# The convolution's sample tokens: products of overlapping rows on GpSimd and sums on VectorE

## The chip, the cores and the metric

The kernel runs on one core of one Trainium2 chip, as one launch. The metric is the device time of that launch in microseconds; the median of several runs counts.

## What is computed

The reference is one inference step of a decoder of two layers. A prompt of 256 tokens and 8 samples of 8 new tokens each go through the same weights. In each layer four groups of 256 channels mix the tokens in four ways: latent attention over cached pages (A), a convolution module (B), spatial gating (C) and a recurrence (D). An output projection, cross-attention to a memory and a feed-forward network follow. The change touches the convolution of group B:

```python
def conv_module(pb, conv_state, p):
    a, gate = pb[..., :CONV_DIM], pb[..., CONV_DIM:]
    glu = a * jax.nn.sigmoid(gate)
    xin = jnp.concatenate([conv_state.astype(glu.dtype), glu], axis=1)
    y = lax.conv_general_dilated(xin, p['conv_w'].astype(xin.dtype)[:, None, :],
                                 window_strides=(1,), padding='VALID',
                                 dimension_numbers=('NWC', 'WIO', 'NWC'),
                                 feature_group_count=CONV_DIM)
    y = y + p['conv_b']
    ...
```

It is depthwise, causal and 31 taps wide. For a sample, xin holds 30 old columns of its state and the 8 new ones, so 38 columns give 8 results per channel.

## The kernel before

Channels lie on the 128 partitions, so the 256 channels of the convolution are two tiles, and the tokens lie along the free dimension: 256 prompt columns and 8 x 8 sample columns, NT = 320 in all. `conv_dense` (line 965) projects and gates. For each of the two tiles it fills `xp`, the prompt's columns with 30 zeros ahead, and `xq`, 8 samples of 38 columns, of which the first 30 come by a DMA of the state (line 972) that depends on nothing else, and the last 8 from the gate. `yi` takes the results. All three are parts of one buffer that the profile calls Bkeep.

`conv` (line 990) is a generator. For each tile it makes 31 steps. A step is one VectorE instruction over the prompt's 256 columns, out of the helper `stt` (line 401), that adds tap k times the shifted `xp` to `yi`, and one over the 64 sample columns (line 1000) that does the same for `xq`. Each of these needs the one before it, since both add into the same columns. The condition `k % 4 < 0` on line 1000 never holds, so all of them are VectorE's. The helper `tt` (line 397) is the plain two-input operation on either engine. `red` (line 416) is a VectorE sum over the last axis, and `hold` says that an instruction is not scheduled ahead of another, without a wait.

The steps of `conv` are run in portions of ten between the steps of `mla_sample` (line 1298), which scores the cached pages of group A. In eight steps that function loads four tiles of pages (Sckt), casts them on ScalarE (Sckh), takes the rest on GpSimd (Sckl, through line 397), multiplies on TensorE (pS, pZ) and goes through a softmax on VectorE (Sra, Sz, Asm). GpSimd also issues indirect DMAs of the page rows (Scb, line 1326). This part of the kernel is called the scoring stage below; it lies at about 205 to 320 us in the first layer and 885 to 1020 us in the second. The convolution's rest (transposes, normalisation, a projection) follows later in the same stage.

The order of each engine's instructions comes from the framework's scheduler. It knows dependences by the columns that an instruction touches, so a tap that reads none of the 8 new columns of `xq` can be placed ahead of the gate. Engines work their queues in order. Each buffer has a fixed count of copies, listed in `BUFS`.

Of the kernel before, what the change touches and what calls it, by code (L numbers as in the profile page):

```python
# [23 lines left out]
NT = 320  # L24
# [297 lines left out]
def body(nc, tc, a, nl=L):  # L322
# [14 lines left out]
                Ckeep=1, Ccv=1, Ck2=2, Csm=4, Ch=2,  # L337
                Bkeep=1, Bms=1, Bf=4, Bg1=4, Bk2=2, Bsm=6, Bh=2, Mm=2, MkT=1, Mvm=2, Mf=2, Mma=1, Mk2=2, Msm=2, Mrw=1)
    PBUFS = dict(D=3, R=2, A=2, S=3, Z=2, K=2, E=2, X=3, Y=2)
# [18 lines left out]
    def block(tag, n):  # L358
        """one tile for what lives as long; returns what hands out its columns"""
        t, used = sb(tag, [128, n]), [0]  # L360

        def take(*shape):
            w = math.prod(shape)
            v = t[:, used[0] : used[0] + w]
            used[0] += w
            assert used[0] <= n
            if len(shape) == 1:
                return v
            d = "abc"[: len(shape)]
            return v.rearrange("p (%s) -> p %s" % (" ".join(d), " ".join(d)), **dict(zip(d, shape)))  # L370

        return take
# [7 lines left out]
    def in_order(first, last):  # L380
        """keeps the streamed products in program order among themselves"""
        after(first, dense_last[0])
        dense_last[0] = last
# [3 lines left out]
    def hold(ins, prev):  # L387
        """not before prev, by the schedule alone"""
        if prev is not None:
            tc.add_manual_dep(ins.ins, prev.ins.name, LATER, reason="held back")  # L390
# [43 lines left out]
    def keep(n):  # L434
        """columns held for the whole launch"""
        o = fixed[0]
        fixed[0] += n
        return fix[:, o : o + n]
# [26 lines left out]
    def rsq(e, now=False):  # L465
        """e <- e ** -0.5"""
        p, n = e.shape
        if n <= 12 and not now:
            tt(e, e, C("mhalf")[:p, :n], ALU.pow, G)
            return  # L470
        z, t = sb("nw", [128, 64]), sb("nw", [128, 64])
        z, t = z[:p, :n], t[:p, :n]
        ts(z.bitcast(I32), e.bitcast(I32), -0.5, 1597463007.0)
        for it in range(3):
            tt(t, z, z, MUL)
            stt(t, t, -0.5, e, MUL, MUL)
            stt(z if it < 2 else e, t, 1.5, z, ADD, MUL)

    def split(hi, lo, src, scale=None, eng=None):
        """hi + lo = src * scale, both in fp32r"""  # L480
        if scale is None:
            S.copy(hi, src)  # L482
            tt(lo, src, hi.bitcast(F32), SUB, eng)
        else:
            act(hi, src, scale=scale)
            stt(lo, src, scale, hi.bitcast(F32), MUL, SUB)

    def halves(raw, spans, scales=None, pool=()):
        """raw: a loaded tile, spans: column ranges -> (hi, lo) for each"""
        out = []  # L490
        per = 512 // (spans[0][1] - spans[0][0])
        for k0 in range(0, len(spans), per):
            part = spans[k0 : k0 + per]
            hi, lo = sb("wh", [128, 512], F32R), sb("wl", [128, 512], F32R)
            c0, c1 = part[0][0], part[-1][1]
            if scales is None:
                split(hi[:, : c1 - c0], lo[:, : c1 - c0], raw[:, c0:c1], None, G if k0 // per in pool else V)
            for n, (a0, a1) in enumerate(part):
                v = slice(a0 - c0, a1 - c0)
                if scales is not None:  # L500
                    split(hi[:, v], lo[:, v], raw[:, a0:a1], scales[k0 + n])
                out.append((hi[:, v], lo[:, v]))
        return out

    def wload(l, nm, idx, K):
        """one chunk of weights: a list of (hi, lo) [128, C] for its K row tiles"""
        o, n = OFFS[(nm, idx)]
        cols = n // K
        raw = sb("wr", [128, 1024])
        nc.sync.dma_start(raw[:, :n], a["w"][l, o : o + 128 * n].rearrange("(p c) -> p c", p=128))  # L510
        return halves(raw, [(k * cols, k * cols + cols) for k in range(K)], None, POOLED.get(nm, ()))
# [77 lines left out]
    def late():  # L589
        """what the first products do not need"""  # L590
        nc.scalar.dma_start(cst[:, EARLY:], a["cst"][:, EARLY:KEPT])
        nc.scalar.dma_start(pti, a["ptab"])
        nc.scalar.dma_start(pt1, a["pt1"])
        for l in range(nl):
            ts(idx[l], pti, 64.0, float(l * 32))
            V.tensor_scalar(out=idx[l], in0=idx[l], scalar1=C("kr"), scalar2=None, op0=ADD)

    def group_norm_T(oj, vec, g, tag="F"):
        """oj: token rows [128, 256] x 3 -> split transposes of the normalised, scaled rows, [128, 2, NT] x 2"""
        r = small(3, 1.0)  # L600
# [7 lines left out]
        out = []  # L608
# [9 lines left out]
    def layernorm64(yj, eps):  # L618
        """per token and 64 columns, in place, without gain"""
        mn, vr = small(12, 0.0), small(12, 1.0)  # L620
# [47 lines left out]
    def rwkv(l, xs, vec):  # L668
# [44 lines left out]
        G.tensor_copy(pT[:, :, 4:12], P[:, :, 263:NT:8])  # L713
        # normalised removal key
        kp = sb("u", [128, 2, NT])
# [24 lines left out]
        stt(b1, ta, 1.0, kk, ADD, MUL)  # L740
        # bonus
        bon = take(12)
# [18 lines left out]
        flat = lambda ap: ap.rearrange("p x t -> p (x t)")  # L761
        # token rows of v, b and k
        UV = [sb("u", [128, 5, 2, 64]) for _ in range(2)]
# [14 lines left out]
        for i in range(2):  # L778
# [11 lines left out]
            gate = S.copy(BKt[i][:, 0:4], p.rearrange("p (c t) -> p c t", c=4))  # L790
        # products between steps of a chunk
        GM = [[sb("u", [128, 5, 128]) for _ in range(2)] for _ in range(2)]
# [13 lines left out]
        for hf in range(2):  # L806
# [4 lines left out]
            for i in range(2):  # L811
                tt(GM[i][hf][:, 4], p[:, i * 128 : i * 128 + 128], mask("mgso" if hf else "mgse"), MUL)
                tt(N[2][R, i, R], GM[i][hf][R, 4, R], ident[R, R], ADD)
        # inverse of the unit triangular blocks by doubling
        v3d = lambda p, n: p[:, : n * 128].rearrange("p (c t) -> p c t", c=n)
# [18 lines left out]
        for lev in (2, 4, 8, 16, 32):  # L834
# [4 lines left out]
            for q in qs:  # L839
# [4 lines left out]
                product(p, Lt[q], Gt[q], n)  # L844
                # the blocks of this level: rows of the first halves, columns of the second
                m = bm(mask("lev%d" % lev), n).rearrange("p n (b x t) -> p n b x t", x=2, t=lev)[:, :, :, 1]
# [17 lines left out]
        lng, lnb = rload(l, ("ln_g", "ln_b"), sb("ln", [128, 512]), back[-1])  # L864
        # state, chunk by chunk
        y = [take(256) for _ in range(3)]
# [77 lines left out]
    def rwkv_out(l, vec, y, lng, lnb, vt, bon, tg, g2):  # L944
        # head norm, bonus, gate
        layernorm64(y, 64e-5)
# [12 lines left out]
    def sigmoid(t, scale=1.0, src=None):  # L959
        """t <- 1 / (1 + exp(scale * src))"""  # L960
        act(t, t if src is None else src, AF.Exp, scale=scale)
# [28 lines left out]
    def conv(l, xpq, vec):  # L990
        (pw,) = mload(l, ("pw",), sb("ms", [128, 512]))
        y = []
        for i, (xp, xq, yi) in enumerate(xpq):
            wc = lambda k: VE(vec, "conv_w", i * 31 + k)
            cb = VE(vec, "conv_b", i)
            ts(yi[:, :256], xp[:, 0:256], wc(0), cb)
            ts(e8(yi[:, 256:NT]), xq[:, :, 0:8], wc(0), cb)
            for k in range(1, 31):
                stt(yi[:, :256], xp[:, k : k + 256], wc(k), yi[:, :256], MUL, ADD)
                (G if k % 4 < 0 else V).scalar_tensor_tensor(out=e8(yi[:, 256:NT]), in0=xq[:, :, k : k + 8], scalar=wc(k), in1=e8(yi[:, 256:NT]), op0=MUL, op1=ADD)  # L1000
                yield
            y.append(yi)
        yj = []
# [98 lines left out]
    def mla(l, pj, vec):  # L1102
# [39 lines left out]
        G.tensor_copy(ckn[LO], pj[2][LO, 192:320])  # L1142
        # queries, keys and values
        rq = take(36)
# [32 lines left out]
        for j in (2, 0, 1):  # L1177
# [24 lines left out]
            else:  # L1202
# [7 lines left out]
                S.copy(kpT[0:32], p[0:32, 256:320])  # L1210
        # sample queries against latents
        qp, qz = take(8, 4, 8), take(8, 4, 32)
# [67 lines left out]
    class Side:  # L1280
        """work that is put between the steps of another"""

# [15 lines left out]
    def mla_sample(l, vec, t, side):  # L1298
# [12 lines left out]
        def scan(g, Q):  # L1311
            """page rows, and their scores without the rotary part"""
            ch[0] = "S"
# [145 lines left out]
    def mem_proj(l, vec, nm, Ms):  # L1459
        """the memory's keys or values; Ms holds its split parts once they are made"""  # L1460
        out = [sb("m" if nm == "wk" else "vm", [128, 512]) for _ in range(2)]
# [76 lines left out]
    def xattn(l, vec, kTm, vm, ahead, nxt):  # L1538
# [4 lines left out]
        for t in qpad:  # L1543
            hold(G.memset(t, 0.0), early)
        # queries without their norms; the sums of squares carry both epsilons
        qT, us = [], sb("m", [128, 2, 4, 4, 8])
# [3 lines left out]
        def scale(c0, n):  # L1550
            """1 / the norms of the queries, with the softmax's factor"""
            r = rs[:, c0 : c0 + n]
# [21 lines left out]
        def sample():  # L1574
# [6 lines left out]
            for g in range(2):  # L1581
# [28 lines left out]
                p = ps("F")  # L1610
                # each head's rows of its own transpose, 128 columns apart
                for h in range(4):
# [154 lines left out]
```

## Time and profile before

| | |
|---|---|
| median of 3 runs | 1382.19 us (1376.61 to 1384.05) |
| span of the profiled execution | 1383.1 us (no time apart from the span is listed) |
| TensorE busy | 1330.9 us, 96% |
| VectorE busy | 962.2 us, 70% |
| ScalarE busy | 651.6 us, 47% |
| GpSimd busy | 217.5 us, 16% |
| granted TensorE clock, mean | 0.970 |

The profile is one execution, taken by the hardware profiler. PE is TensorE, PEld its weight loads, DVE is VectorE, ACT ScalarE and POOL GpSimd. An operand is named by its buffer: Bkeep holds the convolution's columns, fix the constants and tap weights, and names with a small p are in PSUM. Busy time is summed over instructions that do work, and TensorE's ends are modelled. The times of GpSimd are rough. An idle time is put down to the instruction whose signal came last.

### The profile page before, as it was taken

The page shows a single profiled execution, that of the slowest core. Times are in us where ns is not written, and L with a number is a line of the kernel's source. Part 1 is how long each engine was busy: PE and PEld are TensorE (multiplying, and loading weights), DVE is VectorE, ACT ScalarE, POOL GpSimd, SP SyncE. Part 2 cuts the span into 40 slices and gives each one's busy share as a digit, 9 for nine tenths or more (in the row PEclk, how much of TensorE's full clock was granted, in tenths as well). Part 3 has the DMA queues.
Part 4 walks back from the last instruction along what each step waited for, and adds up shares of the span by engine and source line. Part 5 has one row for each costly group of instructions (what it writes and reads, how often), then busy time and mean ns, then how long its engine had stood idle before and what let it go on. Part 6 is the DMA issues. An engine that isn't in the chain of part 4 may idle for free.

```text
span 1383.1 us, 25248 instructions
## 1 busy us (share of the span) xinstructions
PE 1330.9 (96%) x9032; PEld 1113.5 (81%) x9032; DVE 962.2 (70%) x2414; ACT 651.6 (47%) x1425; POOL 217.5 (16%) x280
## 2 busy tenths in 40 slices
PE   5999999999999999999999899999999989999998
PEld 5859765566796799999998597755668959999998
DVE  6879468767786666566786894698777957655663
ACT  4443236667554544434444432375674635442441
POOL 1201313553000000000012113135540000000000
PEclk9999799999999999999999997999999999999999
DMA  7320313454475544444652204134563823444433
GB/s 233 125 77 15 118 44 89 140 159 145 146 253 191 177 157 145 154 153 151 201 171 94 81 11 123 42 88 133 162 215 143 296 93 137 147 144 153 153 115 107
DMA packets 105486, 189.52 MB, mean 137 GB/s; under 512 B 21393, under 2 KB 58642, under 8 KB 105362
## 3 DMA queue, kind: packets, MB, share of 16 engines
q1 hardware_dynamic: 91040, 157.84, 34.6%
q0 software_dynamic: 5120, 20.98, 5.0%
q10 hardware_dynamic: 9202, 9.11, 2.3%
q8 instruction: 71, 1.16, 0.3%
q14 instruction: 53, 0.43, 0.1%
HBM read 182.12 MB, written 5.75 MB: 136 GB/s over the span
## 4 chain that ended last, share of the span: by engine, by line
PE 52%; issue 9%; DVE 2%; POOL 1%; DMA 1%; ACT 0%; SPq 0%; POOLq 0%; ACTq 0%
PE pD L375 38%; PE pR L375 5%; PE pS L375 2%; PE pA L375 2%; PE pZ L375 2%; PE pA L460 1%; DMA Sckt<-in_ckvT 1%; PE pR L460 0%; DVE Bkeep L401 0%; DVE u L401 0%; PE pE L460 0%; POOL Sckl L397 0%; DVE Ccv L401 0%; DVE u L397 0%; DVE Sz L401 0%
## 5 line engine op out<-in xcount | busy, mean ns | idle before, releaser
L482 ACT CAST wh<-wr 128x512 fp32r<-128x512 f32 (+1 forms) x448 | 252.4, 601 | 133.0 <-PE pD L375 83.9
L375 PE MATMUL pD<-Fh,wh 128*128 128x320 f32 x1408 | 310.5, 309 | 0.0
L397 DVE TENSOR_TENSOR wl<-wr,wh 128x512 fp32r<-128x512 f32 (+1 forms) x448 | 291.7, 674 | 11.4 <-ACT wh L482 9.8
L375 PEld LDWEIGHTS pD<-Fh,wh 128*128 128x128 f32 x1408 | 235.7, 188 | 0.0
L375 PE MATMUL pD<-Fh,wl 128*128 128x320 f32 x704 | 217.5, 309 | 0.0
L375 PE MATMUL pD<-u,wh 128*128 128x320 f32 x704 | 154.9, 309 | 0.0
L375 PEld LDWEIGHTS pD<-Fh,wl 128*128 128x128 f32 x704 | 132.2, 188 | 0.0
L375 PEld LDWEIGHTS pD<-u,wh 128*128 128x128 f32 x704 | 117.8, 188 | 0.0
L397 DVE TENSOR_TENSOR Ff<-pD,fix 128x320 f32<-128x320 f32 x88 | 43.2, 491 | 103.3 <-PE pD L375 100.9
L375 PE MATMUL pD<-u,wl 128*128 128x320 f32 x352 | 108.8, 309 | 0.0
L375 PE MATMUL pD<-Nh,wh 128*128 128x320 f32 x384 | 94.6, 326 | 13.8 <-ACT wh L482 13.8
L413 ACT ACTIVATE u<-Ff 128x320 fp32r<-128x320 f32 x44 | 20.8, 472 | 176.1 <-DVE Ff L397 176.1
L397 POOL TENSOR_TENSOR Sckl<-Sckt,Sckh 128x512 fp32r<-128x512 f32 x64 | 85.8, 1351 | 108.7 <-ACT Sckh L1336 91.7
L375 PE MATMUL pS<-Sckh,Auk 128*128 128x512 f32 x256 | 92.0, 432 | 4.3 <-DVE Sra L401 1.8
L413 ACT ACTIVATE Ssq<-pS 128x512 f32<-128x512 f32 x128 | 73.5, 594 | 45.3 <-PE pS L375 38.6
L397 DVE TENSOR_TENSOR fix<-fix,pD 128x320 f32<-128x320 f32 x80 | 38.8, 485 | 73.0 <-PE pD L375 72.3
L375 PEld LDWEIGHTS pD<-Nh,wh 128*128 128x128 f32 x384 | 66.8, 194 | 19.6 <-ACT wh L482 13.8
L375 PEld LDWEIGHTS pS<-Sckh,Auk 128*128 128x128 f32 x256 | 47.3, 197 | 36.4 <-issue 22.1
L401 DVE SCALAR_TENSOR_TENSOR Bkeep<-Bkeep,fix 128x256 f32<-128x256 f32 x120 | 74.5, 624 | 0.6
L1326 POOL DMA_INDIRECT Scb<-in_ckv,fix x64 | 63.4, 991 | 63.4 <-PE pR L375 23.3
L375 PE MATMUL pZ<-Ssq,fix 128*32 128x512 f32 x256 | 71.9, 654 | 1.3 <-ACT Sra L414 0.9
L375 PEld LDWEIGHTS pD<-u,wl 128*128 128x128 f32 x352 | 66.1, 188 | 0.0
(478 smaller groups left out, 2580.7 us busy)
## 6 DMA issues: line engine op xcount, KB each, us to landing
wr<-in_w SPq DMA_DIRECT2D x200, 512.0 KB
Sckt<-in_ckvT SPq DMA_DIRECT2D x256, 64.0 KB
u<-in_memK SPq DMA_DIRECT2D x32, 256.0 KB
u<-in_memV SPq DMA_DIRECT2D x32, 256.0 KB
wr<-in_w SPq DMA_DIRECT2D x16, 384.0 KB
wr<-in_memT SPq DMA_DIRECT2D x12, 256.0 KB
wr<-in_w SPq DMA_DIRECT2D x8, 352.0 KB
Rmk<-in_cst ACTq DMA_DIRECT2D x2, 704.0 KB
```

What stands on the lines that cost most here:

```text
L375: return T.matmul(out, lhsT=lhsT, rhs=rhs, start=start, stop=stop)
L397: return (eng or V).tensor_tensor(out=out, in0=in0, in1=in1, op=op)
L401: return V.scalar_tensor_tensor(out=out, in0=in0, scalar=scalar, in1=in1, op0=op0, op1=op1)
L413: return S.activation(out, in_, func, bias=bias, scale=scale)
L460: T.transpose(out, in_, ident[:n, :n])
L482: S.copy(hi, src)
L1326: ld = nc.gpsimd.indirect_dma_start(out=cb.rearrange("p i c -> p (i c)"), out_offset=None, in_=a["ckv"], in_offset=off)
```

## The change

For the 64 sample columns the 31 steps per tile go. At steps k = 1, 8, 15 and 22 of the prompt's taps, two samples are taken at a time: GpSimd multiplies, for 2 samples x 8 results x 31 taps, the overlapping rows of `xq` with the taps, which are read again for each result, into a new buffer of 496 columns (Bcp), and VectorE sums over the 31 taps into `yi`. The product is held behind the prompt's tap of its step. The bias, which was part of the first tap, is added at the end of the tile. The lines that only drop a comment are left out here.

```diff
@@ BUFS
-                Bkeep=1, Bms=1, Bf=4, Bg1=4, ...
+                Bkeep=1, Bcp=1, Bms=1, Bf=4, Bg1=4, ...
@@ def conv(l, xpq, vec):
             ts(yi[:, :256], xp[:, 0:256], wc(0), cb)
-            ts(e8(yi[:, 256:NT]), xq[:, :, 0:8], wc(0), cb)
             for k in range(1, 31):
-                stt(yi[:, :256], xp[:, k : k + 256], wc(k), yi[:, :256], MUL, ADD)
-                (G if k % 4 < 0 else V).scalar_tensor_tensor(out=e8(yi[:, 256:NT]), in0=xq[:, :, k : k + 8], scalar=wc(k), in1=e8(yi[:, 256:NT]), op0=MUL, op1=ADD)
+                at = stt(yi[:, :256], xp[:, k : k + 256], wc(k), yi[:, :256], MUL, ADD)
+                if k % 7 == 1 and k < 28:
+                    b = 2 * (k // 7)
+                    x0 = xq[:, b : b + 2, 0:8]
+                    win = bass.AP(x0.tensor, x0.offset, list(x0.ap) + [[1, 31]])
+                    taps = VE(vec, "conv_w")[:, i * 31 : i * 31 + 31].unsqueeze(1).unsqueeze(1).to_broadcast([128, 2, 8, 31])
+                    prod = sb("cp", [128, 2, 8, 31])
+                    hold(tt(prod, win, taps, MUL, G), at)
+                    red(yi[:, 256 + 8 * b : 272 + 8 * b].rearrange("p (b t) -> p b t", b=2), prod)
                 yield
+            ts(yi[:, 256:NT], yi[:, 256:NT], cb, op0=ADD)
             y.append(yi)
```

## Rows read from the trace of the kernel before

**Rows 1.** Page, part 1: engines' busy time, share of span, instructions.

```profile
PE 1330.9 (96%) x9032; PEld 1113.5 (81%) x9032; DVE 962.2 (70%) x2414; ACT 651.6 (47%) x1425; POOL 217.5 (16%) x280
```

**Rows 2.** Page, part 2: GpSimd's busy tenths in 40 equal slices.

```profile
POOL 1201313553000000000012113135540000000000
```

**Rows 3.** Busy time by stretch, line 1000 alone: stretch, length, busy (instructions), clock, DMA.

```profile
22.00:70.00 48.00, 10.02 (x44) 0.98 0.50 169
...
660.00:705.00 45.00, 9.79 (x44) 1.00 0.66 221
...
205.00:280.00 75.00, 4.37 (x12) 0.95 0.37 107
...
885.00:980.00 95.00, 3.02 (x11) 0.93 0.37 106
```

**Rows 4.** By stretch: length; PE, PEld, DVE, ACT, POOL busy (instructions); clock, DMA, GB/s.

```profile
22.00:70.00 48.00, 45.28 (x284) 41.22 (x282) 40.11 (x129) 22.32 (x42) 12.00 (x23) 0.98 0.50 169
...
660.00:705.00 45.00, 45.00 (x309) 45.00 (x308) 37.76 (x105) 20.29 (x42) 2.50 (x17) 1.00 0.66 221
...
240.00:280.00 40.00, 39.19 (x318) 23.79 (x314) 32.87 (x69) 23.54 (x52) 23.19 (x21) 1.00 0.42 125
...
280.00:320.00 40.00, 36.54 (x287) 22.80 (x282) 24.61 (x50) 23.36 (x49) 22.58 (x21) 0.91 0.63 177
...
945.00:980.00 35.00, 31.76 (x238) 19.71 (x237) 28.76 (x51) 18.97 (x37) 20.43 (x19) 0.90 0.44 130
```

**Rows 5.** Tile Bkeep, both tap forms: duration ns min/median/max, first and last start.

```profile
L1000 DVE SCALAR_TENSOR_TENSOR Bkeep<-Bkeep,fix x120: 265/276/1379, 22.8 to 968.9; 128x64 f32<-128x64 f32 x120
...
L401 DVE SCALAR_TENSOR_TENSOR Bkeep<-Bkeep,fix x120: 443/475/3360, 175.7 to 985.1; 128x256 f32<-128x256 f32 x120
```

**Rows 6.** VectorE's groups, whole span: busy us, mean ns of one, idle before.

```profile
L418 DVE TENSOR_REDUCE Asm<-Sra 128x1 f32<-128x512 f32 x16 | 10.8, 676 | 0.1
```

**Rows 7.** GpSimd's groups, 205 to 320 us.

```profile
L397 POOL TENSOR_TENSOR Sckl<-Sckt,Sckh 128x512 fp32r<-128x512 f32 x28 | 37.3, 1342 | 45.7 <-ACT Sckh L1336 36.4 <-DMA Sckt<-in_ckvT 8.3 <-ACT Ch L413 0.7
```

**Rows 8.** Timelines, VectorE and GpSimd: start us, length us, instruction, count.

```profile
205.60 4.12 POOL L397 TENSOR_TENSOR Sckl<-Sckt,Sckh 128x512 fp32r<-128x512 f32 x3
...
205.65 1.52 DVE L397 TENSOR_TENSOR Rkeep<-Rkeep,Rsm 128x256 f32<-128x256 f32 x1
...
207.10 0.67 DVE L418 TENSOR_REDUCE Asm<-Ak 128x4 f32<-128x512 f32 x1
...
1008.70 1.99 DVE L397 TENSOR_TENSOR wl<-wr,wh 128x512 fp32r<-128x512 f32 x1
```

**Rows 9.** Timeline of VectorE, a prompt tap beside GpSimd work.

```profile
947.59 3.36 DVE L401 SCALAR_TENSOR_TENSOR Bkeep<-Bkeep,fix 128x256 f32<-128x256 f32 x1
```

**Rows 10.** Chain of waits, 886 to 1029 us: start us, length us, what.

```profile
947.67 3.28 DVE Bkeep L401
...
951.81 2.83 DVE Ccv L401 x2
...
954.64 1.40 DVE Ccv L397
...
995.93 2.21 DVE Sz L401
```

**Rows 11.** Timelines: the last prompt tap (VectorE), TensorE taking the convolution's result.

```profile
288.52 0.47 DVE L401 SCALAR_TENSOR_TENSOR Bkeep<-Bkeep,fix 128x256 f32<-128x256 f32 x1
...
319.69 0.66 PE L460 MATMUL pE<-fix,Bkeep 128*128 128x128 f32 x4
```

**Rows 12.** Busy time by stretch, all engines; the granted clock stands ahead of DMA.

```profile
210.00:215.00 5.00, 3.97 (x20) 2.21 (x18) 5.00 (x18) 4.71 (x21) 0.00 (x0) 1.00 0.38 101
...
215.00:220.00 5.00, 4.12 (x35) 3.03 (x35) 3.85 (x14) 4.00 (x11) 1.28 (x1) 0.81 0.17 49
...
220.00:225.00 5.00, 5.00 (x14) 2.13 (x14) 5.00 (x22) 1.89 (x5) 1.26 (x1) 0.51 0.49 137
...
140.00:160.00 20.00, 20.00 (x91) 12.83 (x90) 7.12 (x16) 2.67 (x8) 4.96 (x5) 0.50 0.37 110
```

More of the change, by code (lines that the diff above doesn't have):

```diff
@@ L337, in body @@
                 Ckeep=1, Ccv=1, Ck2=2, Csm=4, Ch=2,
-                Bkeep=1, Bms=1, Bf=4, Bg1=4, Bk2=2, Bsm=6, Bh=2, Mm=2, MkT=1, Mvm=2, Mf=2, Mma=1, Mk2=2, Msm=2, Mrw=1)
+                Bkeep=1, Bcp=1, Bms=1, Bf=4, Bg1=4, Bk2=2, Bsm=6, Bh=2, Mm=2, MkT=1, Mvm=2, Mf=2, Mma=1, Mk2=2, Msm=2, Mrw=1)
     PBUFS = dict(D=3, R=2, A=2, S=3, Z=2, K=2, E=2, X=3, Y=2)
```

## Prediction

> **What bounds the kernel now.** I read the page's engine shares first [rows 1]: TensorE is busy 96% of the span and VectorE 70%. The slices [rows 2] then show when GpSimd is at work: it has two stretches, the 5th to the 10th slice and the 25th to the 30th, one per layer. Their later parts are the stages in which the cached pages are scored, and the convolution's prompt taps run as filler there. So a change to the convolution is worth what it does in about 205 to 320 us and 885 to 1020 us, and nothing where TensorE is full and VectorE has time over.
>
> Next I asked where the 120 sample taps of the old line 1000 run [rows 3]. The reader should see that 44 of each layer's 60 run far ahead of the convolution: 44 in 22 to 70 us and 44 in 660 to 705 us. Their windows lie wholly in the old state, which a DMA brings early, so the scheduler pulls them forward. Only 12 and 11 run in the scoring stages, and 9 just ahead of these. The table of stretches by engine [rows 4] says what these places are worth. In 660 to 705 TensorE is busy 45.00 of 45 us, so taking 9.8 us from VectorE gives nothing. In 22 to 70 it is busy 45.28 of 48, so all that could be gained is 2.7 us. In the scoring stages TensorE still is busy for over nine tenths, but VectorE is at 32.87 of 40 and 28.76 of 35: there the two nearly share the limit.
>
> **What is removed.** 120 taps of 0.276 us median [rows 5] and 4 first taps: 33 us of VectorE in the sum. By place: 88 taps, 19.8 us [rows 3], lie under TensorE and I count them at nothing; their cover is the TensorE work just named, and without it they would be worth 2.7 us at most in the first layer and 0 in the second. In the scoring stages 23 taps go, 4.37 + 3.02 = 7.4 us [rows 3].
>
> **What is added on VectorE.** 16 sums of 128x496 into 128x16, four per tile of 128 channels, two tiles, two layers. The nearest row is a reduction of 128x512 at 676 ns [rows 6]; I take 0.68 us. The new product reads all 38 columns of two samples, the new ones included, so it can't run ahead as the old taps did. It is held behind prompt taps 1, 8, 15 and 22. The prompt taps of the first tile begin in the dense stage ahead of the scoring and those of the second lie wholly in it, so I put 2 of 8 products per layer ahead of the scoring stage and 6 in it: 12 sums, 12 x 0.68 = 8.2 us. Four additions of the bias over 64 columns cost at most one tap each, 4 x 0.276 = 1.1 us.
>
> **What is added on GpSimd, and what it does to VectorE.** 16 products of 128x496. The nearest row is the split of 128x512, 1342 ns [rows 7], 28 of them in 205 to 320 us; 16 x 1.34 = 21.5 us in all, 12 x 1.34 = 16.1 us in the scoring stages. GpSimd is busy 23.19 and 22.58 us of 40 there [rows 4], so time is free; I count its own queue at nothing, and its cover is that idle time. The price is elsewhere. Rows of VectorE that start while GpSimd multiplies or subtracts are stretched [rows 8]: with GpSimd at 205.60 for 4.12 us, a VectorE product of 128x256 takes 1.52 us, while the reduction at 207.10, with one input, takes its usual 0.67. A prompt tap has a median of 475 ns [rows 5] and takes 3.36 us at 947.59 [rows 9]. I took each VectorE row of the two scoring stages less the median of its form and kept those over 0.4 us: 35 rows, the first at 205.65 and the last at 1008.70 [rows 8], 43.2 us in sum (19.5 and 23.7). 59 two-input GpSimd operations lie in these stages, so each costs VectorE 43.2 / 59 = 0.73 us. Twelve more cost 8.8 us. The bounds: 0 if only sums and readers of PSUM happen to fall under a product, 1.34 if VectorE always stands for the whole of it (16.1 us); a product of this four-dimensional pattern could also be slower than a plain one, and at twice the length the 8.8 become 17.6. I take the mean, since prompt taps, which are of the kind that is stretched, are what stands next to these products.
>
> The Trainium skill has a rule on this (SBUF — State Buffer, Who interferes with whom): a VectorE instruction with two SBUF inputs and a GpSimd instruction that reads SBUF exclude each other, and the one that comes second waits for the whole of the other, while a reduction never does. The trace agrees on which rows are stretched. By the full wait the twelve products would cost 16.1 us instead of 8.8, and the time would be 1389 us instead of 1386.
>
> **The sum.** VectorE in the two scoring stages: 8.8 + 8.2 + 1.1 - 7.4 = +10.7 us. How much of that reaches the end is read from the chain of waits in the second layer's scoring stage [rows 10]: of its 23.7 us of stretching, the chain holds the pieces at 947.67 (2.8 us over its median), 951.81 (2.0), 954.64 (1.1) and 995.93 (1.6), 7.5 us or 32%. So 0.32 x 10.7 = +3.4 us, and the end of the convolution itself has room: its last tap ends at 289 us and TensorE takes its result at 319.69 [rows 11]. The profiled span is 1383.1 us; plus 3.4 gives 1386.5. The page lists no time of that execution apart from its span, which is 0.9 us above the median of the three runs, 1382.19; I subtract half a microsecond for that and say 1386. Bounds of the sum: with no pass-through and the 2.7 us of the start gained, 1380; with everything passed on, and products of twice the length, 1383 + 10.7 + 8.8, or 1403.
>
> **The wait that is new.** Each sum waits for its product, on VectorE, in order. Behind it stand prompt taps, the maxima and rescalings of the attention, and the weight splits; ScalarE's exponentials and TensorE's transposes wait for those. GpSimd's queue is in order too: a product stands behind splits that wait for ScalarE's casts, 36.4 us over 9 waits in 205 to 320 [rows 7], a mean of 4.0.
>
> **Rivals.**
> - *VectorE stands at the sums (slower).* If half of the twelve sums are queued right behind a product that itself stands behind such a split, VectorE loses 6 x 4.0 = 24 us; at 32% that is +7.7, with the 3.4 above 1394 us, and up to 1407 if these waits are not covered at all. It decides from about two such sums per layer. For it: the queues are in order, and GpSimd's long waits are real. Against: six of the eight products have only filler around them, and the scheduler orders them by when it thinks the product is done.
> - *TensorE's clock (slower).* The granted clock falls to 0.51, its lower level of 1.2 GHz, in 220 to 225 us, after two stretches in which TensorE was busy only 3.97 and 4.12 of 5 us [rows 12]. Such a stretch costs 2.4 us, with the 0.9 of the stretch before it 3.4. One more in each layer would give 1386.5 + 6.8, or 1393.
> - *The new order heals a slow stretch (faster).* In 140 to 160 us the clock is at 0.50 for the whole stretch [rows 12], 10 us lost, behind the small products of the recurrence. VectorE, 10 us lighter in 22 to 70 us, may let other work fall there. Without that loss: 1386.5 - 10, about 1376, and with a like gain in layer two 1366. For it: every engine's order is laid out anew. Against: in 130 to 160 us VectorE isn't what TensorE waits for.
> - *It doesn't do what it says.* The 31 dependent taps were not what anybody waited for: 88 of 120 were out of the way already. That is part of the forecast; if in addition the stretching falls on covered work, the time stays at 1383.
>
> **How the numbers follow.** A measurement of this kernel can tell about 0.5% (6.9 us) from no change, so the bounds are 1375.3 and 1389.1. Chances: the forecast with its own spread of 1380 to 1389, the last rival's 1383 included, 0.48; VectorE at the sums 0.25; the clock falling more often, or products of twice the length with most passed on, 0.12; the healed stretch 0.15. So faster 0.15, same 0.48, slower 0.37. The range 1374 to 1403 takes in the bounds of the sum (1380 to 1403); it leaves out the far half of the faster case and what of the sums' waits is passed on in full, somewhat under 0.2.
>
> **What would show it.** Right: no sample products of VectorE in 22 to 70 us and TensorE's busy time there unchanged; 16 GpSimd products of near 1.3 us; more stretched prompt taps beside them; VectorE busier in the scoring stages by about 5 us per layer. Wrong: products of 2.5 us or more; VectorE's idle time ahead of the sums put down to GpSimd in microseconds each; a different count of half-clock stretches; or TensorE finishing the first 140 us clearly earlier.

## The result, and the profile after

The changed kernel takes 1404.35 us (median of 4 runs, 1396.96 to 1408.96) where the kernel before took 1381.21 (4 runs, 1376.61 to 1384.05). The ratio is 1.0155, with a 95% interval of 1.012 to 1.019: it is slower by about 23 us. The profiled execution is its shortest, 1396.96 us with a span of 1395.2; the spans of the four runs are 1395.2, 1407.1, 1398.0 and 1407.2 us at mean granted clocks of 0.971, 0.962, 0.968 and 0.962.

The page of after: its span, part 1, and GpSimd's slices of part 2 (they answer to [rows 1, 2]).

```profile
span 1395.2 us, 25117 instructions
...
PE 1332.6 (96%) x9032; PEld 1116.5 (80%) x9032; DVE 955.7 (68%) x2310; ACT 654.5 (47%) x1425; POOL 237.8 (17%) x296
...
POOL 1202324653000000000012122335540000000000
```

VectorE has 104 instructions and 6.5 us less, GpSimd 16 instructions and 20.3 us more, TensorE the same 9032 matmuls. The next rows, of after, are the busy time of all engines by stretch, with the columns of [rows 4].

```profile
22.00:70.00 48.00, 45.31 (x287) 41.21 (x288) 32.78 (x88) 23.21 (x43) 9.87 (x23) 1.00 0.52 157
660.00:705.00 45.00, 45.00 (x309) 45.00 (x309) 27.83 (x58) 19.04 (x39) 2.71 (x17) 1.00 0.63 202
...
240.00:280.00 40.00, 38.98 (x321) 23.98 (x321) 35.99 (x65) 24.22 (x55) 25.59 (x23) 1.00 0.41 124
280.00:320.00 40.00, 36.04 (x302) 24.79 (x299) 25.75 (x53) 23.66 (x48) 23.46 (x22) 0.91 0.60 168
```

In the first two lines VectorE is 7.3 and 9.9 us lighter than in [rows 4] and TensorE is where it was, 45.31 against 45.28 and 45.00 against 45.00. In 240 to 280 VectorE is 3.1 us heavier. Neither stretch alone shows 23 us. For the whole of both scoring stages I read two wider stretches in each kernel. Here they are for before, and then for after, in the same columns.

```profile
175.00:365.00 190.00, 181.18 (x1289) 115.75 (x1288) 141.66 (x353) 113.50 (x269) 68.64 (x67) 0.95 0.41 119
860.00:1070.00 210.00, 200.18 (x1458) 135.50 (x1458) 160.08 (x392) 120.37 (x281) 73.58 (x70) 0.97 0.42 126
```

```profile
175.00:365.00 190.00, 177.17 (x1262) 115.19 (x1262) 145.29 (x339) 111.15 (x264) 77.73 (x73) 0.94 0.39 113
860.00:1070.00 210.00, 195.52 (x1403) 128.94 (x1404) 155.57 (x359) 116.74 (x276) 83.93 (x78) 0.96 0.36 108
```

TensorE is busy 381.36 of these 400 us before and 372.69 after: its idle time grows from 18.6 to 27.3 us, it gets 82 matmuls fewer done in the same two stretches, and the granted clock is 0.01 lower in both. (Idle here is the length of the two stretches less the busy time.) GpSimd's power operations on small tiles, one of a name in each layer, mark the stages. From the one on Rsm to the one on Bsm, which holds the scoring stage, it takes 137.2 us instead of 127.1 in the first layer and 138.8 instead of 128.5 in the second. The part ahead of that, back to the power operation on Asm, is shorter, 132.9 instead of 139.2 us and 134.4 instead of 136.3; everything else stays within about 2 us. So in the profiles the scoring stages lose 20 us and the parts ahead of them give 8 back, which makes the 12 us between the spans.

A second way to split the loss needs only each run's span and mean clock. Span x (1 - clock) is the time that the clock withheld, and span x clock is the rest. In the four runs of after the rest hardly moves (1353.3 to 1354.7), while the withheld time does (40.5 to 53.5). In the two profiles the withheld time is equal, 41.5 and 40.5 us, and the rest went from 1341.6 to 1354.7. In the medians both grew: withheld 49.1 against 35 to 37 before, rest 1353.7 against 1340 to 1344. So by this account the 23 us are some 10 to 13 us of rest and some 12 to 14 us of clock. The rest is in the main TensorE's waiting: over the two profiled spans its idle time goes from 52.2 to 62.6 us. The share of the clock is an upper bound, since it also counts clock that was withheld while TensorE stood idle, and only the medians show it, not the two profiles.

Now the new instructions. The two groups on the tile Bcp, of after: durations in ns (least, median, longest), first and last start.

```profile
L397 POOL TENSOR_TENSOR Bcp<-Bkeep,fix x16: 1157/1191/1484, 172.4 to 986.0; 128x496 f32<-128x496 f32 x16
L420 DVE TENSOR_REDUCE Bkeep<-Bcp x16: 648/656/670, 175.8 to 989.0; 128x16 f32<-128x496 f32 x16
```

The group of the sums in VectorE's groups over the whole span, of after, with the idle time ahead of it last:

```profile
L420 DVE TENSOR_REDUCE Bkeep<-Bcp 128x16 f32<-128x496 f32 x16 | 10.5, 657 | 0.0
```

VectorE never stood at a sum: 0.0 us of idle time ahead of 16. What the products do to it can be seen in one place. Three excerpts of after's timelines (GpSimd, VectorE, TensorE: start us, length us, instruction, and in brackets the idle time before it and what ended it), around one product of the first layer.

```profile
278.92 2.52 POOL L397 TENSOR_TENSOR Sckl<-Sckt,Sckh 128x512 fp32r<-128x512 f32 x2
...
282.58 1.17 POOL L397 TENSOR_TENSOR Bcp<-Bkeep,fix 128x496 f32<-128x496 f32 x1
...
286.17 1.29 POOL L397 TENSOR_TENSOR Sckl<-Sckt,Sckh 128x512 fp32r<-128x512 f32 x1
```

```profile
278.10 6.99 DVE L401 SCALAR_TENSOR_TENSOR Bkeep<-Bkeep,fix 128x256 f32<-128x256 f32 x6
285.01 0.66 DVE L420 TENSOR_REDUCE Bkeep<-Bcp 128x16 f32<-128x496 f32 x1
285.59 2.16 DVE L401 SCALAR_TENSOR_TENSOR Bkeep<-Bkeep,fix 128x256 f32<-128x256 f32 x1
287.67 0.68 DVE L401 SCALAR_TENSOR_TENSOR Sra<-pZ,Sra 128x512 f32<-128x512 f32 x1
```

```profile
288.49 1.07 PE L375 MATMUL pZ<-Ssq,fix 128*32 128x512 f32 x8 [2.02 <-DVE Sra L401]
290.88 1.19 PE L375 MATMUL pS<-Sckh,Auk 128*128 128x512 f32 x2 [1.32 <-DVE Asm L401]
```

Six prompt taps take 6.99 us instead of six times 0.48, one beside two splits and one beside the product; the next stands 2.16 us beside another split; the softmax's Sra comes behind them in VectorE's queue, and TensorE stands 2.02 us for it. The pieces of the chain of waits there, of after (start us, length us, what):

```profile
278.61 3.14 DVE Bkeep L401
...
282.30 1.76 DVE Bkeep L401
...
285.59 2.16 DVE Bkeep L401
```

So the prompt's taps are links of the chain here; some were before, too, as the piece at 947.67 us in [rows 10]. Their share of the chain in 886 to 1066 us of the second layer is 7.4% (13 us) after and 2.5% (4.5 us) before. The two are not quite alike: in before 37 us of that chain are put to "issue", for which the profile shows no wait, and in after 8 us.

### The profile page after: what moved, and what is told of

Same layout as the page of the kernel before. It is cut to its first block, busy times and chain, and to the rows that moved or that the text cites. A ratio compares the mean times of both kernels' runs of the same rounds, so it can differ in the third digit from the quotient of the medians.

```text
span 1395.2 us, 25117 instructions
## 1 busy us (share of the span) xinstructions
PE 1332.6 (96%) x9032; PEld 1116.5 (80%) x9032; DVE 955.7 (68%) x2310; ACT 654.5 (47%) x1425; POOL 237.8 (17%) x296
## 4 chain that ended last, share of the span: by engine, by line
PE 86%; DVE 8%; ACT 2%; issue 1%; POOL 1%; DMA 1%; SPq 0%; ACTq 0%; POOLq 0%; DVEq 0%
PE pD L375 51%; PE pR L375 10%; PE pA L375 6%; PE pS L375 6%; PE pZ L375 5%; PE pK L375 3%; DVE Bkeep L401 2%; PE pA L460 2%; PE pX L375 1%; PE pY L375 1%; PE pE L375 1%; PE pR L460 1%; PE pE L460 1%; DVE u L401 1%; PE pX L460 0%
## 5 line engine op out<-in xcount | busy, mean ns | idle before, releaser
L375 PE MATMUL pS<-Sckh,Auk 128*128 128x512 f32 x256 | 96.1, 449 | 4.2 <-DVE Asm L401 3.3
L401 DVE SCALAR_TENSOR_TENSOR Bkeep<-Bkeep,fix 128x256 f32<-128x256 f32 x120 | 82.1, 686 | 1.0
L375 PE MATMUL pZ<-Ssq,fix 128*32 128x512 f32 x256 | 67.0, 622 | 7.0 <-DVE Sra L401 4.3
```

The lines of the kernel that those rows point to most:

```text
L375: return T.matmul(out, lhsT=lhsT, rhs=rhs, start=start, stop=stop)
L401: return V.scalar_tensor_tensor(out=out, in0=in0, scalar=scalar, in1=in1, op0=op0, op1=op1)
```

## The experiments

Three theories went into them. *Stretch*: GpSimd's products hold VectorE's two-input operations up. *Load*: the sums, and what else VectorE does now in the scoring stages, cost it. *Order*: the scheduler lays out every engine's queue anew, and a new order leaves TensorE more or less idle whatever the work is. Ratios are to the kernel before, run in the same rounds on the same chip, with 95% intervals. "Idle" is TensorE's in the two wide stretches above (before 18.6 us).

**Products on VectorE, same places** (a_dve).

```diff
-                    hold(tt(prod, win, taps, MUL, G), at)
+                    hold(tt(prod, win, taps, MUL), at)
```

> The changed kernel with the 16 products on VectorE instead of GpSimd: no GpSimd instruction is added over the kernel before, VectorE gets 16 x 0.68 = 11 us more. Stretch: the stretching of about 9 us goes and the products cost about as much, so 1404 within 4, with VectorE's prompt taps back at a mean near 0.62 us. Load: VectorE has 8 us more in the scoring stages, so slower, about 1412. Order: not to be told beforehand; the time goes with TensorE's idle time and granted clock and not with VectorE's busy time.

1381.96 us, ratio 1.0003 (0.9978 to 1.0027). The 16 products take VectorE 664 ns each, so it has 10.6 us more to do than in after, and the kernel is 22.4 us faster. The wide stretches of this kernel, in the same columns:

```profile
175.00:365.00 190.00, 179.14 (x1291) 116.04 (x1289) 147.64 (x352) 112.08 (x269) 70.36 (x67) 0.96 0.40 118
860.00:1070.00 210.00, 202.13 (x1488) 138.40 (x1488) 167.50 (x398) 122.96 (x289) 76.12 (x70) 0.98 0.39 120
```

TensorE idles 18.7 us, as before, and does 1488 matmuls in the second stretch where after does 1403, while VectorE is busier than in after. From 32 us ahead of the operation on Rsm to the one on Bsm, VectorE is busy 254.5 us here, 256.4 in after and 240.9 in before, over both layers: about after's load, and none of its loss. Load alone, as a theory, falls here. Stretch missed as well in the size that it gave: it had priced the products on VectorE at what the stretching costs, and expected after's 1404 within 4.

**Products one tap later** (a_shift), then this edit together with the one of a_dve (a_shift_dve), and both kinds once more at taps 4, 11, 18, 25 (a_s4, a_s4_dve).

```diff
-                if k % 7 == 1 and k < 28:
+                if k % 7 == 2 and k < 28:
```

> The changed kernel with its four products and sums per tile behind prompt taps 2, 9, 16 and 23 instead of 1, 8, 15 and 22; the same work, the same engines. Three theories of the 23 us that the change cost. Stretch: the GpSimd products stretch VectorE's two-input instructions; then this kernel takes what the changed one takes, 1404 us, within 4. Load: VectorE's sums now lie in the scoring stages where they can't be covered; also 1404 within 4. Order: what costs is the order in which the scheduler lays out all the rest, and where TensorE then stands; then a small shift of the products moves the time by more than 6 us, either way.

> The changed kernel with products behind prompt taps 2, 9, 16, 23 as in a_shift, and on VectorE as in a_dve. It makes a pair with a_shift (1391 us) that differs in the engine of the products alone. GpSimd products cost (stretch): faster than a_shift by 5 to 22 us, 1370 to 1386. Order alone: no relation; as likely slower than a_shift as faster.

> The changed kernel with its products, on GpSimd, behind prompt taps 4, 11, 18, 25. A third place for the same work, after 1404 (taps 1, 8, 15, 22) and 1391 (one tap later). GpSimd products cost: above the kernel before in any place, 1386 to 1405. Order alone: spread about the kernel before, 1375 to 1395.

> As a_s4, with the products on VectorE. GpSimd products cost: faster than a_s4 by 5 us or more and near the kernel before, 1378 to 1386. Order alone: no relation to a_s4.

Three pairs result, each with products of the same place on the one or the other engine:

| products behind taps | GpSimd | VectorE | difference | of it rest | of it clock | TensorE idle | stretching | softmax waits |
|---|---|---|---|---|---|---|---|---|
| 1, 8, 15, 22 (after, a_dve) | 1404.35 | 1381.96 | 22.4 | 11.5 | 10.5 | 27.3 and 18.7 | 49.8 and 42.2 | 8.3 and 2.7 |
| 2, 9, 16, 23 | 1391.10, 1.0052 (1.0029 to 1.0076) | 1378.35, 0.9994 (0.9967 to 1.0022) | 12.7 | 3.4 | 10.7 | 25.3 and 20.1 | 52.2 and 39.6 | 8.1 and 2.5 |
| 4, 11, 18, 25 | 1386.61, 1.0043 (1.0014 to 1.0072) | 1377.65, 0.9975 (0.9944 to 1.0006) | 9.0 | 7.0 | 3.0 | 26.3 and 18.9 | 53.7 and 37.5 | 7.6 and 0.8 |

Rest and clock are differences of the medians of span x clock and span x (1 - clock), which do not add up exactly, and before's own rest is 1343.8 us in the rounds of a_shift and 1340.2 in those of a_shift_dve, so the 3.4 of the second pair can't be told from nothing. Stretching is summed over VectorE's instructions of 175 to 345 and 865 to 1045 us: the time of each less the median of its operation and form, where that is over 0.4 us. Before has 42.2 us of it. The last column is what TensorE waits, in the two wide stretches, for rows that write Sra, Sz or Asm, the softmax of the pages; the longest of these waits on VectorE, of after and then of a_dve, first and second layer (us in total, times, longest):

```profile
PE pZ L375 <- DVE Sra L401: 2.0, 1, 2.0
PE pS L375 <- DVE Asm L401: 1.9, 2, 1.3
...
PE pZ L375 <- DVE Sra L401: 2.3, 2, 2.1
PE pS L375 <- DVE Asm L401: 1.3, 1, 1.3
```

```profile
PE pS L375 <- DVE Asm L401: 1.3, 1, 1.3
...
PE pS L375 <- DVE Asm L401: 0.9, 1, 0.9
```

In every pair GpSimd's products cost time (22.4, 12.7 and 9.0 us by the medians; 21, 8 and 9 by the ratios) and 5 to 9 us of TensorE's idling. But moving them by one tap alone gave back 13 us, so the place, or the order that goes with it, matters as much as the engine; stretch and load had both expected 1404 within 4 there. And the pair with the least added stretching (7.6 us, against 12.6 and 16.2) has the largest cost, so the amount of stretching is not what sets it. TensorE's waits for the softmax are 5.6 to 6.8 us longer with the products on GpSimd, about as much as the added idling. Before has 6.6 us of them too, though, at the time of the faster kernels, so they alone don't mark a slow one. None of these three kernels with products on VectorE can be told from before.

**A fill in place of the product** (a_memset): GpSimd is as busy, VectorE waits for it in the same places, but nothing is read.

```diff
-                    hold(tt(prod, win, taps, MUL, G), at)
+                    hold(G.memset(prod, 0.0), at)
+                    G.memset(prod, 0.5)
```

> The changed kernel with each product replaced by two GpSimd fills of the same 496 columns (so the samples' convolution is a constant); a fill writes and reads nothing. GpSimd is held for about as long (two fills of near 0.5 us) and the sums wait for it as before. If what costs is the reading of two inputs beside VectorE's (stretch): no VectorE row is longer under a fill, and the time is that of the kernels without GpSimd products, 1380 to 1392. If what costs is GpSimd's queue, in which page splits stand behind the products: 1400 or more, as the changed kernel.

1383.58 us, ratio 1.0029 (1.0001 to 1.0056), idle 21.4 us. The fills, of this kernel:

```profile
L1006 POOL MEMSET Bcp<- x16: 501/512/657, 172.7 to 981.7; 128x496 f32 x16
```

Two of them are 1.02 us, near the product's 1.19. The same queue and the same new wait cost 4 us where the product cost 23 (by the intervals 0.1 to 8 against 17 to 26); so the wait of the sums for GpSimd is not what costs, as far as one new order can tell. The stretching of VectorE is 45.1 us here, 42.2 before and 49.8 after. The prompt's taps are 6.8% of the chain in 886 to 1066 us here, nearly the 7.4% of after, so their share of the chain doesn't tell the slow kernel from the other.

**The products without the sums** (a_nosum): 16 columns of the product are copied in place of its sum.

```diff
-                    red(yi[:, 256 + 8 * b : 272 + 8 * b].rearrange("p (b t) -> p b t", b=2), prod)
+                    V.tensor_copy(yi[:, 256 + 8 * b : 272 + 8 * b].rearrange("p (b t) -> p b t", b=2), prod[:, :, :, 0])
```

> The changed kernel with each sum of 128x496 replaced by a copy of 16 columns, so the sample tokens get tap 0's product alone; the products stay on GpSimd and are waited for as before. Stretch: stays at 1404 within 4, since the products are all there. Load: 12 sums of 0.5 us less in the scoring stages, 6 us, so about 1398 if all of it counts. Order: moves by more than 6 us or not at all, with no relation to the 6 us.

1402.26 us, ratio 1.0145 (1.0098 to 1.0192). A copy takes 166 ns where the sum took 656, 7.8 us less for VectorE, and the intervals of this kernel and after lie over each other: nothing that these runs can tell came back. It isn't the same loss, however. The rest is 1348.8 us, 4.9 less than in after, and the clock withholds 51.8 us, the most of all kernels; the stretching is only 44.2 us, the waits for the softmax 4.2, and here VectorE stands 3.7 us at two copies for their products, which it never did at a sum of after. A like time thus came by another way, which the theory of stretch alone doesn't give.

**The sums without the products** (a_sums): the sum reads the overlapping rows themselves.

```diff
-                    hold(tt(prod, win, taps, MUL, G), at)
-                    red(yi[:, 256 + 8 * b : 272 + 8 * b].rearrange("p (b t) -> p b t", b=2), prod)
+                    hold(V.tensor_reduce(out=yi[:, 256 + 8 * b : 272 + 8 * b].rearrange("p (b t) -> p b t", b=2), in_=win, op=ALU.add, axis=AX.X), at)
```

> The changed kernel with no products at all: the 16 sums read the overlapping rows themselves, so the samples' convolution has all taps equal to one. VectorE has the same sums in the same places as in the changed kernel, GpSimd has nothing added, and no sum waits for GpSimd. If the products on GpSimd are what costs: between a_none's 1391 and the kernels with products on VectorE, 1376 to 1391. If the sums cost: 1398 or above.

1398.78 us, ratio 1.0112 (1.0057 to 1.0168). This is the miss that matters most: no product is on GpSimd, the stretching is 40.1 us, less than before's, VectorE does less than in a_dve, and it is some 15 us slower than before and than a_dve. Idle 23.6 us, withheld 46.8. Its expectation had put 1398 or above to the sums. But a_dve has the same sums in the same places, and the products besides, without a loss, and a_nosum had none of them and was as slow as after. So something other than the products can cost about two thirds as much, and the new order is what is left of the three theories.

**No sample convolution** but its first tap and the bias (a_none).

```diff
+            ts(e8(yi[:, 256:NT]), xq[:, :, 0:8], wc(0), cb)
...
-                if k % 7 == 1 and k < 28:
+                if False:
...
-                    red(yi[:, 256 + 8 * b : 272 + 8 * b].rearrange("p (b t) -> p b t", b=2), prod)
...
-            ts(yi[:, 256:NT], yi[:, 256:NT], cb, op0=ADD)
```

> The sample tokens' convolution is left out but for tap 0 with the bias (one VectorE instruction per tile): no products, no sums. It takes 7 us of VectorE out of the scoring stages of the kernel before and 18 us out of those of the changed one. Stretch and load: about 1379, a little under the kernel before's 1381. Order: with no sample work left at all it may still be slower than the kernel before, 1385 or more, if the layout of the rest is what costs.

1391.40 us, ratio 1.0062 (1.0039 to 1.0085). With all of the work in question gone, the kernel is slower than before. So leaving out the 33 us of taps that the change set out to remove gained nothing in the order that came of it, and an order without them can be worse by 9 us than the order with them. What they are worth in an unchanged order is not shown.

**The old taps in the scoring stage** (b_inplace): the kernel before, with each sample tap held behind its prompt tap.

```diff
-                stt(yi[:, :256], xp[:, k : k + 256], wc(k), yi[:, :256], MUL, ADD)
-                (G if k % 4 < 0 else V).scalar_tensor_tensor(out=e8(yi[:, 256:NT]), in0=xq[:, :, k : k + 8], scalar=wc(k), in1=e8(yi[:, 256:NT]), op0=MUL, op1=ADD)
+                at = stt(yi[:, :256], xp[:, k : k + 256], wc(k), yi[:, :256], MUL, ADD)
+                hold((G if k % 4 < 0 else V).scalar_tensor_tensor(out=e8(yi[:, 256:NT]), in0=xq[:, :, k : k + 8], scalar=wc(k), in1=e8(yi[:, 256:NT]), op0=MUL, op1=ADD), at)
```

> The kernel before with each sample tap held behind the prompt tap of its step, so that the 88 taps that ran in 22 to 70 us and 660 to 705 us run in and just ahead of the scoring stages, on VectorE, with no GpSimd instruction added. VectorE's load there counts: 88 taps at a pitch of 0.20 us are 18 us more in these stages, at a third to all of it 1387 to 1399. Only the GpSimd products cost (VectorE's filler is covered): 1376 to 1386, like the kernels with products on VectorE.

1389.36 us, ratio 1.0058 (1.0028 to 1.0088). All 120 taps lie in 175 to 365 and 860 to 1070 us now. The 88 that came are 88 x 0.276 = 24.3 us by their median length, and the time is 8.0 us longer: 0.33 of it reaches the end. That is no firm price of VectorE's time there. VectorE as a whole is only 13.9 us busier in the two wide stretches (315.7 against 301.7), by which it would be 0.58, and a_dve, 13.4 us busier there, lost nothing.

**No splits on GpSimd** (b_split): the kernel before, with all 64 page splits on VectorE.

```diff
-                lows.append(tt(lo, ck, hi.bitcast(F32), SUB, G if j in [0, 1, 2, 3] else V))
+                lows.append(tt(lo, ck, hi.bitcast(F32), SUB, G if j in [] else V))
```

> The kernel before with all 64 splits of the cached pages on VectorE instead of GpSimd. No two-input GpSimd instruction is left in the scoring stages but a few small ones. Stretch: the 43 us of stretched VectorE rows go nearly to zero, the splits add 64 x 0.6 = 38 us, so VectorE's busy time there hardly changes and the time stays within 1375 to 1388. Load (the nominal VectorE work is what counts): 38 us more, 1395 or above.

1380.89 us, ratio 0.9990 (0.9961 to 1.0020). VectorE's groups in 175 to 345 us: of before first, then of this kernel (busy us, mean ns of one, idle before it).

```profile
L401 DVE SCALAR_TENSOR_TENSOR Bkeep<-Bkeep,fix 128x256 f32<-128x256 f32 x60 | 34.6, 579 | 0.3
```

```profile
L401 DVE SCALAR_TENSOR_TENSOR Bkeep<-Bkeep,fix 128x256 f32<-128x256 f32 x60 | 28.6, 477 | 0.0
L397 DVE TENSOR_TENSOR Sckl<-Sckt,Sckh 128x512 fp32r<-128x512 f32 x29 | 19.6, 683 | 0.6 <-issue 0.4 <-ACT Ssq L413 0.2
```

And the first of these groups in after and in a_memset:

```profile
L401 DVE SCALAR_TENSOR_TENSOR Bkeep<-Bkeep,fix 128x256 f32<-128x256 f32 x59 | 39.3, 669 | 0.5
```

```profile
L401 DVE SCALAR_TENSOR_TENSOR Bkeep<-Bkeep,fix 128x256 f32<-128x256 f32 x59 | 37.5, 637 | 0.6
```

Without two-input operations on GpSimd there is no stretching left: 0.0 us in both stages, a tap at 477 ns mean, its median. VectorE took 64 splits of 0.68 us, 43.7 us, and lost 42.2 us of stretching; the time didn't move. That the stretching comes from GpSimd's two-input operations is shown, and also that all 42.2 us of it can be traded for as much VectorE work without a loss or a gain in the time. The equal time is a sum of two changes, though: the rest is 1349.7 us against 1344.2 for before in the same rounds, and the withheld time 29.7 against 37.3.

**Products and sums behind the last prompt tap** (a_late), with VectorE, to put them out of the attention's way.

```diff
-                if k % 7 == 1 and k < 28:
...
+        for i, (xp, xq, yi) in enumerate(xpq):
+            for b in (0, 2, 4, 6):
...
+                hold(tt(prod, win, taps, MUL), at)
+                red(yi[:, 256 + 8 * b : 272 + 8 * b].rearrange("p (b t) -> p b t", b=2), prod)
+                yield
...
```

> Products on VectorE, and products and sums of both tiles behind the last prompt tap, so from about 285 us on in the first layer, where VectorE was busy 24.6 us of 40 in the kernel before, and not in 205 to 280 where it was busy over four fifths. If VectorE's place in the scoring stage decides: faster than the places before it (1382, 1378, 1378), 1368 to 1377. If the convolution's end becomes what TensorE waits for: 1385 or above, with TensorE idle ahead of the convolution's transposes.

1395.44 us, ratio 1.0098 (1.0073 to 1.0124). It is the slowest with products on VectorE: idle 30.2 us, the rest at 1355.4, the clock as before (37.6 withheld). Its time is in the range expected if TensorE came to wait for the convolution's end, but that wait isn't there: for rows of Bg, which the convolution's tail writes, TensorE waits 3.2 us in the wide stretches, and 4.4 in a_dve. It waits 10.0 us for the softmax instead of 2.7. No kernel here is shown to be faster than before.

## Why the prediction was right or wrong

**Right: where the work lay.** The 88 early taps were counted at nothing for TensorE's sake, and its busy time there is the same to 0.03 us. That the 31 dependent taps were not what anybody waited for fits a_none, which leaves them out and gains nothing, though in another order.

**Right: the terms of VectorE's sum.** Products took 1.19 us (1.34 taken), sums 0.656 (0.68), two of eight products per layer began ahead of the scoring (172.4 and 184.4 us in the first), the stretching grew by 49.8 - 42.2 = 7.6 us (8.8 taken; the prediction's own count of before gave 43.2). Over the 15 products that lie in these stretches that is 0.51 us each, where 0.73 was taken. The Trainium skill's rule of the whole wait (SBUF — State Buffer, Who interferes with whom) would have made it 17.9 for the 15, with the measured length. On what is not stretched the rows agree with it: the sums took 648 to 670 ns, and no row beside fills alone was longer by over 0.4 us. But more is stretched than the rows with two inputs, which the prediction named: a row with one input, on Bsm at 275.26 us of before, took 1.27 us where 0.16 is the median, and three copies of a_nosum took 1.23 to 1.25 us instead of 0.17, each beside splits. VectorE's busy time between the operations on Rsm and Bsm, with the 32 us ahead of them, grew by 15.6 us over both layers (240.9 to 256.4) where 10.7 were forecast; the stretches are also 20 us longer. With the pass-through of 0.32 that is 5.0 us instead of 3.4.

**Wrong: that the sum was the change.** The likeliest time was 1386 us, faster or slower by little; it became 1404.35, 1.35 us over the upper end of the range, and slower had a chance of 0.37 in all. The step that failed is the one that made VectorE's balance times 0.32 the whole forecast, with "its own spread of 1380 to 1389", and left everything else of the order and the clock as it was. The balance came out near the forecast, and it doesn't set the time: with 256.4 us of VectorE in the stages after takes 1404.35, and with 254.5 a_dve takes 1381.96. Nor was 0.32 well founded, since 14 us of the chain that it was read from are "issue". What the runs showed in its place is 8.7 us more idling of TensorE in the scoring stages, and in the medians 12 to 14 us more of withheld clock. Put as a term: with the prediction's 0.73 us a product and the 664 ns that one takes on VectorE, moving the 12 products of the stages there trades 8.8 us of stretching for 12 x 0.66 = 8.0 us of work, 0.3 us at 32%. Measured, it was 22.4, 12.7 and 9.0 us. The term of the products on GpSimd was mis-sized by that much. One way in which it costs is seen: a stretched tap ahead of a softmax row holds TensorE's next product, as the timelines at 278 to 291 us show. That the clock's share follows from it is not shown; in the two profiles the withheld time is equal.

**The rivals.** VectorE standing at the sums, at 0.25 the first of them, didn't happen: 0.0 us ahead of the sums, and a_memset keeps the wait and loses the cost. The clock, inside the 0.12 and priced at 6.8 us, is the one that came true in part: by the medians up to half of the 23 us is withheld clock (49.1 against 35 to 37 us), more than its price, and beside it came the idling of TensorE, which that rival didn't have. The healed stretch came in small part: 140 to 160 us has a granted clock of 0.58 instead of the 0.50 of [rows 12], which is 1.6 of the 6.4 us that the first layer gained ahead of its scoring, and the scoring lost more. The new order was weighed only in this faster direction; it has two sides, and here the slower one is the more frequent. Of 13 variants 9 lie above before and have an interval that leaves out 1 (after, a_shift, a_s4, a_nosum, a_none, a_memset, b_inplace, a_sums, a_late), and none lies so below it. Five of the nine have new work on GpSimd and b_inplace has more of VectorE's in the stages, so a_none, a_sums and a_late are the ones that speak for the order.

**What stays open.** GpSimd's products cost time in three pairs out of three, and a_memset suggests that it is their reading. But across the pairs the cost falls as the stretching rises, a_nosum is as slow as after with little stretching, and a_sums, with no product on GpSimd, is slower than before by some 15 us. So how much of the 23 us is the products' stretching in bad places, and how much an order that would be slow with any work in it, isn't settled: an order can't be held while the work in it changes, since the scheduler lays it out from both. That the new order is the cause in a_sums and a_none is what is left over, not what a run showed by itself.

## What to carry to other kernels

Ask of removed work whether anybody waited for it, and in a kernel whose order a scheduler lays out, give the re-laying a term of its own: here edits that added nothing to GpSimd moved the time by -0.25%, which is not clear of noise, to +1.1%. A two-input operation handed to an idle GpSimd is not free work: beside a VectorE that does two-input operations it cost VectorE 0.51 us each in after and 0.66 in b_split, where VectorE would have needed 0.66 to 0.68 us for it; the other kernels with products lie between 0.13 (a_nosum) and 0.77 (a_s4). Run the same edit at two or three places and on both engines before believing that either the edit or its place is the cause.

## What the runs showed of the hardware

- The overlapping, repeating four-dimensional read was no slower on GpSimd, column for column: 1191 ns for 496 columns, 2.40 ns a column, against 1342 ns for 512 plain ones [rows 7], 2.62. The prediction's upper end, twice the length, was far off. VectorE's product of this pattern took 664 ns, and its sum straight from the overlapping rows 658.
- Three prompt taps that meet a GpSimd operation end about 0.3 us after it, whether it takes 1.17 us or 2.52: 278.61 + 3.14 is 0.31 us after the end of two splits in a row, 282.30 + 1.76 is 0.31 after the end of the product, 285.59 + 2.16 is 0.29 after the end of a split. In all three the tap's recorded start lies ahead of GpSimd's, by 0.28 to 0.58 us, so the recorded starts of this profile don't tell which of the two goes first; GpSimd's are rough.
- Splitting a run's time into span x clock and span x (1 - clock) shows two kinds of scatter: 25 runs of before had 1339 to 1348 us of the first, and 27.5 to 45.8 us of the second.
